# Tracing the merge's last gated sums ahead of the weight splits that follow them

## The chip, the cores and the metric

The kernel runs on one core of a Trainium2 chip. The metric is device time in microseconds (us), the median over several executions. One further execution is recorded by the profiler; its timeline is what "the trace" means below. The engines are PE (matrix multiply), DVE (vector), ACT (scalar), POOL, and SP, which here issues the transfers. Each works through its own queue in order.

## The reference, cut to what matters

Two layers over 256 tokens of width 1024, in float32. The part that the change touches is the merge of the two attention branches and the projection behind it:

```
branch_a = (o_gla * silu(gg)) @ w_o_gla
branch_b = gqa_attention(q, k, v) @ w_o_attn
mixed = sigmoid(gate_a) * branch_a + sigmoid(gate_b) * branch_b
h = h + rms_norm(mixed @ w_out, g_mix_post)
gate, up = split(rms_norm(h, g_ffn_pre) @ w_ffn_in, 2)
h = h + rms_norm((silu(gate) * up) @ w_ffn_out, g_ffn_post)
```

Each token half (`hf`, 128 tokens) and each column half (`j`, 512 columns) of `mixed` is one block of 128x512.

## The kernel before, in words

Weights stream through one pipeline (`Stream`, lines 214 to 324). A unit is 512 rows by 512 columns, 1 MB. SP loads it into one of two raw buffers. It is then split into a rounded high part (`wh`, a cast on ACT, line 113) and the rest (`wl`, a subtraction on DVE, line 109), each in two pieces of 128x1024; the two parts have four places each. A matrix product is three matmuls, high by high, high by low and low by high (`mm3`, line 99). `ws.take()` hands the next split unit to the matmuls. `ws.done()` gives its place back and, through `fill` (line 309), at once traces the split of the next loaded unit and the load behind it: two casts, two subtractions, and the transfers into the raw buffer that the split frees.

The merge runs over the steps in `MERGE` (line 39). Its last four steps are the `w_o_gla` units: for column half j = 0 the row halves kh = 0 and 1, then the same for j = 1. One unit is 24 matmuls, 12 for hf 0 and then 12 for hf 1. After kh = 1 the function `merged` (line 1204) takes each half's sum from PSUM: a multiplication by the gate (line 106) and an addition of the other branch (line 1210), both 128x512 on DVE. For j = 1 it also makes a task that will transpose the block on PE (line 436) and split the transposed block for the next product (`transpose_in`, line 432: a cast on ACT, a subtraction on DVE). A task waits for a number of ticks, and a tick falls after every six matmuls; here the number is `WAIT_MIX` = 3.

Next comes the product with `w_out` (`by_half`, line 662), first all of hf 0 and then all of hf 1. Its four units are called out 0 to out 3 here: (kh 0, j 0), (kh 0, j 1), (kh 1, j 0), (kh 1, j 1). Out 0 and out 1 need the merged blocks with j = 0, out 2 and out 3 those with j = 1. With four places, out 0 and out 1 are split into the places of the first two gla units, and out 2 and out 3 into those of the last two. The splits of out 2 and out 3 bring the loads of the first two units of `w_ffn_in` with them, two transfers each.

The order on each engine is not the traced order as it stands. A planner goes over the traced instructions with a clock of its own, in which every instruction and transfer has an estimated duration, and gives each engine the instruction that is ready and was traced first. `tc.high_priority(AHEAD)` counts the instructions in its block as traced 400 places earlier. `tc.issue_after(x)` puts what its block traces on x's engine behind x in that engine's queue, and leaves other engines' instructions free.

Of the kernel before, what the change touches and what calls it, by code (L numbers as in the profile page):

```python
# [15 lines left out]
ALU = mybir.AluOpType  # L16
# [9 lines left out]
AHEAD, EMPTY, EMPTY_FIRST = 400, 100, 1600  # L26
# [25 lines left out]
def trunk_kernel(ctx: ExitStack, tc: tile.TileContext, a: dict, out: bass.AP):  # L52
# [7 lines left out]
    nc = tc.nc  # L60
# [23 lines left out]
    def acc():  # L84
        return accp.tile([P, 512], F32, tag="acc", name=nm("acc"))
# [19 lines left out]
    def vmul(out, in0, in1):  # L105
        nc.vector.tensor_tensor(out=out, in0=in0, in1=in1, op=ALU.mult)
# [107 lines left out]
    class Stream:  # L214
# [8 lines left out]
        def __init__(self, depth):  # L223
            self.depth, self.held, self.room, self.ready, self.open = depth, 0, 0, [], False
            self.loads, self.jobs, self.lend = [], [], False
            pairs = {}
            for item in plan:
                if callable(item):
                    x = Load(item)
                    self.loads.append(x)  # L230
                    self.jobs.append(lambda x=x: self.plain(x))
                else:
                    units, n = item
                    if n == 1:
                        b11, b12, b21, b22 = units
                        x, z = (Load(b, lambda tag=tag: self.lent(tag), tag == "wh") for b, tag in ((b11, "wh"), (b12, "wl")))
                        y, q = Load(b22, big), Load(b21)
                        pairs[id(units)] = x, y, z, q
                        self.loads += [x, y, z]
                    if n == 5:  # L240
                        self.loads.append(q)
                    self.jobs.append(lambda p=pairs[id(units)], n=n: self.step(n, *p))
# [83 lines left out]
    ws = Stream(4)  # L326
# [105 lines left out]
    def transpose_in(sp, src, k, n, hf, plain=None):  # L432

        ps = aux()
        for i in range(n):
            nc.tensor.transpose(ps[:, i * P : (i + 1) * P], src[:, i * P : (i + 1) * P], ident)
        with tc.high_priority(AHEAD):
            sp.put(ps[:, : n * P], k, n, hf * P, P)
        if plain is not None:
            nc.scalar.copy(plain, ps[:, : n * P])  # L440
# [100 lines left out]
    def amode(o, sp, hf, k0, w, first, last, c0=0):  # L541

        wh, wl = (t[:, :2048].rearrange("p (k c) -> p k c", c=512)[:, :, c0 : c0 + o.shape[-1]] for t in w)
        sp.need(hf, k0)
        for k in range(4):
            mm3(o, sp.tok(k0 + k, hf), (wh[:, k, :], wl[:, k, :]), first and k == 0, last and k == 3)
            if k % 2 and (k == 3 or o.shape[-1] == 512):
                tick()
# [95 lines left out]
    def project_t(sp):  # L644

        o = [acc(), acc()]
        for kh in range(2):
            wmode(o, sp, kh * 4, ws.take(), kh == 0, kh == 1)
            ws.done()
        return o  # L650

    def project(sp):

        o = [acc(), acc()]
        for kh in range(2):
            w = ws.take()
            for hf in range(2):
                amode(o[hf], sp, hf, kh * 4, w, kh == 0, kh == 1)
            ws.done()
        return o  # L660
# [74 lines left out]
    uT = Split()  # L735
# [71 lines left out]
    for l in range(DEPTH):  # L807
# [86 lines left out]
        o = {}  # L894
# [135 lines left out]
        for x in range(2):  # L1030
            o = project_t(uT)
# [143 lines left out]
        for j in range(2):  # L1175
            o = project(uT)
            for hf in range(2):
                nc.scalar.copy(gg[:, hf, j * 512 : (j + 1) * 512], o[hf])
        gT = Split()
# [21 lines left out]
        mixT, sgate, seen = Split(), [], set()  # L1201
        part_of = lambda br, hf, j: sgate[br][:, hf, j * 512 : (j + 1) * 512]

        def merged(br, hf, j, o):
            vmul(part_of(br, hf, j), o, part_of(br, hf, j))
            if (hf, j) not in seen:
                seen.add((hf, j))
                return
            y = part_of(0, hf, j)
            nc.vector.tensor_tensor(out=y, in0=y, in1=part_of(1, hf, j), op=ALU.add)  # L1210

            def turn():
                yield WAIT_MIX
                transpose_in(mixT, y, 4 * j, 4, hf)

            turn = turn() if j or hf == 0 else mixT.turn_words(y, 0, 4, hf)
            mixT.makers[hf].append(Task(turn, part[0], j))

        def units(sp, then):
            for j in range(2):  # L1220
                o = [acc(), acc()]
                for kh in range(2):
                    w = ws.take()
                    for hf in range(2):
                        amode(o[hf], sp, hf, kh * 4, w, kh == 0, kh == 1)
                    ws.done()
                    if kh == 1:
                        for hf in range(2):
                            then(hf, j, o[hf])
                    yield  # L1230

# [10 lines left out]
        def gated(hf, o0, o1):  # L1242
            merged(1, hf, 0, o0)
            merged(1, hf, 1, o1)

        gate_units, gla_units, seven_ = gates(), units(gT, lambda hf, j, o: merged(0, hf, j, o)), None
        for x in MERGE:
            if x == "g" and not ogate.over:
# [43 lines left out]
        for hf in range(2):  # L1292
            ws.lend = hf == 1
            for b in range(2):
                o = acc()
# [39 lines left out]
        o = []  # L1335
# [69 lines left out]
        for hf in range(2):  # L1405
            s = slice(hf * P, (hf + 1) * P)
            for j in range(2):
                o = acc()
# [35 lines left out]
        uT = nxt  # L1444
# [47 lines left out]
```

## Time and profile before

| | |
|---|---|
| time before, median of 3 | 925.68 us (925.47 to 928.27) |
| the profiled execution's own time | 931.57 us |
| its span, first to last instruction | 929.8 us |
| PE busy | 908.2 us, 98% of the span |
| DVE busy | 768.4 us, 83% |
| ACT busy | 642.7 us, 69% |
| mean granted clock of PE | 0.995 |
| share of the 16 DMA engines | 58.8% |

PE's busy time includes matmuls that run at a lower clock. A view of waits names the engine and the line that waited, what it waited for, and the time in total, how often, and the longest. A timeline row gives start, duration, engine, line, operation, output <- inputs, and in brackets the idle time before it with what ended it. In tile names the digit is the layer: `big_0gate` is the merged block of layer 0, `aux_0merge` its transposed copy in PSUM, `wl_0merge<-raw_0merge` a weight split traced in the merge.

### The profile page before, as it was taken

Reading aid. Unit: us, or ns where it says so; the run is one execution under the profiler, and the core shown is the slowest. Engines: PE = TensorE matmul, PEld = TensorE weight load, DVE = VectorE, ACT = ScalarE, POOL = GpSimd, SP = SyncE. Lnnn points to the kernel's source line nnn. Section 1 sums busy time; section 2 is a strip of 40 time slices with the busy share of each in tenths; the row PEclk is TensorE's granted clock in tenths of the full one; section 3 lists DMA queues with packets and bytes.
Section 4 is the critical chain, followed back from the end, with each engine's and each line's share of the span. In section 5 each row is a group of like instructions: output and inputs, shape, how many; then the busy total and the mean of one; then the engine's idle time right before and its main releaser. Section 6 shows DMA issues by size and latency. Waiting matters only on the chain.

```text
span 929.8 us, 12251 instructions
## 1 busy us (share of the span) xinstructions
PE 908.2 (98%) x4561; PEld 769.7 (83%) x4561; DVE 768.4 (83%) x963; ACT 642.7 (69%) x1032; POOL 87.7 (9%) x150
## 2 busy tenths in 40 slices
PE   8999999999899999999999999999989999999996
PEld 6999888888688887888899988888878788888786
DVE  4798978987578998998689789798785799979874
ACT  4668778864477787677765686777555788858563
POOL 2600211040010000000122002200001000000000
PEclk9999999999999999999999999999999999999999
DMA  6564456757477675847555524394583866665551
GB/s 227 173 213 149 137 176 230 156 187 241 132 232 230 175 257 173 290 145 242 173 181 182 183 89 155 119 270 157 206 257 111 283 206 222 212 249 169 181 182 46
DMA packets 117786, 176.60 MB, mean 190 GB/s; under 512 B 33047, under 2 KB 56087, under 8 KB 117726
## 3 DMA queue, kind: packets, MB, share of 16 engines
q1 hardware_dynamic: 117726, 175.81, 58.8%
q8 instruction: 36, 0.59, 0.3%
q14 instruction: 24, 0.20, 0.1%
HBM read 167.41 MB, written 1.05 MB: 181 GB/s over the span
## 4 chain that ended last, share of the span: by engine, by line
PE 58%; DVE 18%; DMA 10%; ACT 7%; issue 4%; POOL 2%; SPq 0%; ACTq 0%; POOLq 0%; DVEq 0%
PE acc_0ffnin L97 9%; PE acc_1ffnin L97 6%; PE acc_0ffnin L577 4%; DVE wl_1ffnin L109 4%; PE acc_1gate L97 4%; PE acc_1gqk L97 2%; PE acc_0rq L97 2%; PE acc_0gqk L97 2%; PE acc_1ple L97 2%; PE acc_1gg L97 2%; PE acc_1v L97 2%; PE acc_0v L97 2%; PE acc_0gg L97 2%; DVE wl_0merge L109 2%; DMA raw_1ffnin<-in_w_ffn_out_dram 2%
## 5 line engine op out<-in xcount | busy, mean ns | idle before, releaser
L97 PE MATMUL acc_1ffnin<-wh_1ffnin,big_1ffnin 128*128 128x512 f32 x176 | 56.3, 392 | 0.0
L97 PE MATMUL acc_0ffnin<-wh_0ffnin,big_0ffnin 128*128 128x512 f32 x176 | 56.2, 391 | 0.0
L113 ACT CAST wh_1ffnin<-raw_1ffnin 128x1024 fp32r<-128x1024 f32 x38 | 38.4, 1050 | 19.0 <-DMA raw_1ffnin<-in_w_ffn_out_dram 12.9
L109 DVE TENSOR_TENSOR wl_1ffnin<-raw_1ffnin,wh_1ffnin 128x1024 fp32r<-128x1024 f32 x38 | 45.1, 1222 | 7.9 <-ACT wh_1ffnin L113 7.9
L109 DVE TENSOR_TENSOR wl_0ffnin<-raw_0ffnin,wh_0ffnin 128x1024 fp32r<-128x1024 f32 x38 | 45.0, 1222 | 6.6 <-ACT wh_0ffnin L113 6.6
L113 ACT CAST wh_0ffnin<-raw_0ffnin 128x1024 fp32r<-128x1024 f32 x38 | 38.3, 1049 | 17.2 <-DMA raw_0ffnin<-in_w_ffn_out_dram 10.5
L97 PEld LDWEIGHTS acc_1ffnin<-wh_1ffnin,big_1ffnin 128*128 128x128 f32 x176 | 33.0, 188 | 7.0 <-DVE big_1ffnin L109 0.2
L97 PEld LDWEIGHTS acc_0ffnin<-wh_0ffnin,big_0ffnin 128*128 128x128 f32 x176 | 33.0, 188 | 6.9 <-DVE big_0ffnin L109 0.2
L113 ACT CAST wh_1ffnin<-lent_1ffnin 128x1024 fp32r<-128x1024 f32 x30 | 30.2, 1050 | 9.7 <-DVE lent_1ffnin L292 4.0
L109 DVE TENSOR_TENSOR wl_1ffnin<-lent_1ffnin,wh_1ffnin 128x1024 fp32r<-128x1024 f32 x30 | 35.4, 1222 | 1.3 <-ACT wh_1ffnin L113 1.3
L109 DVE TENSOR_TENSOR wl_0ffnin<-lent_0ffnin,wh_0ffnin 128x1024 fp32r<-128x1024 f32 x30 | 35.4, 1223 | 1.2 <-ACT wh_0ffnin L113 1.2
L113 ACT CAST wh_0ffnin<-lent_0ffnin 128x1024 fp32r<-128x1024 f32 x30 | 30.2, 1051 | 8.8 <-PE acc_0ffnin L97 3.4
L97 PE MATMUL acc_0ffnin<-wl_0ffnin,big_0ffnin 128*128 128x512 f32 x88 | 34.5, 392 | 0.3 <-DVE wl_0ffnin L109 0.2
L97 PE MATMUL acc_1ffnin<-wl_1ffnin,big_1ffnin 128*128 128x512 f32 x88 | 34.5, 393 | 0.1
L577 PE MATMUL acc_1ffnin<-wh_1ffnin,mid_1ffnin 128*128 128x512 f32 x96 | 31.0, 390 | 0.0
L577 PE MATMUL acc_0ffnin<-wh_0ffnin,mid_0ffnin 128*128 128x512 f32 x96 | 31.0, 390 | 0.0
L97 PE MATMUL acc_1ffnin<-wh_1ffnin,big_1wout 128*128 128x512 f32 x96 | 30.4, 389 | 0.0
L97 PE MATMUL acc_0ffnin<-wh_0ffnin,big_0wout 128*128 128x512 f32 x96 | 30.3, 389 | 0.0
L97 PE MATMUL acc_0rq<-wh_start,big_start 128*128 128x384 f32 (+1 forms) x96 | 25.2, 347 | 1.2 <-ACT big_start L124 1.2
L97 PE MATMUL acc_1rq<-wh_0ple,big_0ple 128*128 128x384 f32 (+1 forms) x96 | 23.4, 325 | 0.0
L577 PE MATMUL acc_1ffnin<-wh_1ffnin,big_1wout 128*128 128x512 f32 x72 | 23.1, 389 | 0.0
L577 PE MATMUL acc_0ffnin<-wh_0ffnin,big_0wout 128*128 128x512 f32 x72 | 23.1, 389 | 0.0
(741 smaller groups left out, 3027.3 us busy)
## 6 DMA issues: line engine op xcount, KB each, us to landing
raw_0ffnin<-in_w_ffn_out_dram SPq DMA_DIRECT2D x11, 1024.0 KB, 5.3
raw_1ffnin<-in_w_ffn_out_dram SPq DMA_DIRECT2D x11, 1024.0 KB, 5.7
lent_0ffnin<-in_w_ffn_in_dram SPq DMA_DIRECT2D x6, 1024.0 KB, 7.5
lent_1ffnin<-in_w_ffn_in_dram SPq DMA_DIRECT2D x6, 1024.0 KB, 7.5
raw_0rq<-in_w_in_dram SPq DMA_DIRECT2D x4, 1024.0 KB, 5.1
raw_0v<-in_w_in_dram SPq DMA_DIRECT2D x4, 1024.0 KB, 5.0
raw_0merge<-in_w_out_dram SPq DMA_DIRECT2D x4, 1024.0 KB, 5.8
raw_0wout<-in_w_ffn_in_dram SPq DMA_DIRECT2D x8, 512.0 KB, 4.7
```

What stands on the lines that cost most here:

```text
L97: return nc.tensor.matmul(o, lhsT, rhs, start=start, stop=stop)
L109: nc.vector.tensor_tensor(out=out, in0=in0, in1=in1, op=ALU.subtract)
L113: cast = nc.scalar.copy(hi, src)
L577: nc.tensor.matmul(o, x, y, start=first and k + n == 0, stop=k == 3 and n == 2, skip_group_check=not first)
```

## The change

For the second column half (j = 1) of the gla product, the multiplication and addition in `merged` are counted as traced 400 places earlier. `merged` returns the addition. `ws.done()` for the unit (kh 0, j 1) is no longer called after its own matmuls, but after hf 0's twelve matmuls of (kh 1, j 1) and hf 0's `merged`; the one for (kh 1, j 1) comes after hf 1's `merged`. Both are called under `issue_after` of the addition just traced, so the subtractions of out 2's split queue behind hf 0's addition, and those of out 3's split behind hf 1's. Hf 0's task is made twelve matmuls earlier, so its three ticks also begin twelve matmuls earlier. The gate units (`uT`) and j = 0 are traced as before.

```diff
         def merged(br, hf, j, o):
-            vmul(part_of(br, hf, j), o, part_of(br, hf, j))
+            y = part_of(0, hf, j)
+            with tc.high_priority(AHEAD) if br == 0 and j else nullcontext():
+                vmul(part_of(br, hf, j), o, part_of(br, hf, j))
+                if (hf, j) in seen:
+                    added = nc.vector.tensor_tensor(out=y, in0=y, in1=part_of(1, hf, j), op=ALU.add)
             if (hf, j) not in seen:
                 seen.add((hf, j))
                 return
-            y = part_of(0, hf, j)
-            nc.vector.tensor_tensor(out=y, in0=y, in1=part_of(1, hf, j), op=ALU.add)
...
             mixT.makers[hf].append(Task(turn, part[0], j))
+            return added
...
                     for hf in range(2):
                         amode(o[hf], sp, hf, kh * 4, w, kh == 0, kh == 1)
-                    ws.done()
-                    if kh == 1:
-                        for hf in range(2):
+                        if j and kh and sp is gT:
+                            with tc.issue_after(then(hf, j, o[hf]).ins):
+                                ws.done()
+                    if not j or sp is uT:
+                        ws.done()
+                        for hf in range(2 * kh):
                             then(hf, j, o[hf])
                     yield
```

## The prediction

> **What bounds the kernel now.** I read the waits of PE first, since PE is busy nearly all the time and any wait of PE that is left must be on the path to the end.
>
> ```profile
> core 0 of [0], span 929.8 us
> engine line waited for: us in total, times, longest us
> PE aux_0merge L436 <- DVE big_0gate L1210: 4.2, 2, 3.2
> PE aux_1merge L436 <- DVE big_1gate L1210: 3.0, 1, 3.0
> PE warm L124 <- POOL ident masks.py:199: 1.5, 1, 1.5
> ```
>
> The two largest waits are the ones that the change is about: the transposes (L436) wait for the addition (L1210) of the merge, in each layer. The list is sorted, so every other group of waits is 1.5 us or less, and that one lies at the start. Nothing of size stands later at which an earlier PE would be held up. Next I read PE's timeline at these places.
>
> ```profile
> 224.49 0.60 PE L436 MATMUL aux_0merge<-ident,big_0gate 128*128 128x128 f32 x4
> 224.85 0.48 PE L97 MATMUL acc_0merge<-wh_0merge,big_0gg 128*128 128x512 f32 x1
> 225.16 0.39 PE L97 MATMUL acc_0merge<-wl_0merge,big_0gg 128*128 128x512 f32 x1
> ...
> 231.76 0.39 PE L97 MATMUL acc_0wout<-wh_0merge,big_0merge 128*128 128x512 f32 x1
> ...
> 237.04 0.66 PE L436 MATMUL aux_0merge<-ident,big_0gate 128*128 128x128 f32 x4 [1.04 <-DVE big_0gate L1210]
> 240.89 1.05 PE L436 MATMUL aux_0merge<-ident,big_0gate 128*128 128x128 f32 x4 [3.19 <-DVE big_0gate L1210]
> ...
> 687.23 0.39 PE L97 MATMUL acc_1wout<-wh_1merge,big_1merge 128*128 128x512 f32 x1
> ...
> 691.32 0.60 PE L436 MATMUL aux_1merge<-ident,big_1gate 128*128 128x128 f32 x4
> 694.97 1.11 PE L436 MATMUL aux_1merge<-ident,big_1gate 128*128 128x128 f32 x4 [3.05 <-DVE big_1gate L1210]
> ```
>
> In layer 1, 18 matmuls of the `w_out` product start between 687.23 and 691.32: 4.09 / 18 = 0.227 us each. Then hf 0's block is transposed, and at the same tick hf 1's, which waits 3.05 us. Layer 0 waits 1.04 and 3.19. An undisturbed set of four transposes costs PE 0.44 us: from 224.49 two matmul steps end at 225.16, 0.67 later, of which one step of 0.227 is the matmul's own. The set at 240.89 takes 1.05 instead of 0.60, so something follows the wait, and the third view shows what. Its columns after the stretch are its length, the busy time (and count) of PE, PE's weight loads, DVE, ACT and POOL, then the granted clock, the DMA share and GB/s.
>
> ```profile
> 231.70:237.00 5.30, 4.30 (x19) 3.22 (x18) 4.18 (x6) 4.10 (x5) 0.00 (x0) 1.00 0.74 232
> 241.00:243.00 2.00, 2.00 (x7) 1.73 (x8) 0.84 (x2) 0.59 (x1) 0.00 (x0) 0.50 0.78 197
> 243.00:245.00 2.00, 2.00 (x7) 1.60 (x6) 0.29 (x1) 0.00 (x0) 0.00 (x0) 0.65 0.94 315
> 245.00:247.00 2.00, 2.00 (x10) 1.64 (x10) 0.00 (x0) 0.00 (x0) 0.00 (x0) 1.00 0.04 12
> 695.00:697.00 2.00, 2.00 (x7) 1.80 (x8) 1.38 (x3) 0.82 (x2) 0.00 (x0) 0.50 0.78 207
> 697.00:699.00 2.00, 2.00 (x7) 1.54 (x7) 0.43 (x1) 0.00 (x0) 0.00 (x0) 0.65 0.98 340
> ```
>
> After each long wait PE runs at half clock, and for a while counts as fully busy. The loss is 2 x 0.50 + 2 x 0.35 = 1.7 us a layer. The short wait of 1.04 us (first row) left the clock at 1.00. So the price of the stall is larger than the waits: 1.04 + 3.19 + 1.7 = 5.9 us in layer 0, 3.05 + 1.7 = 4.75 in layer 1, together **10.7 us**.
>
> Why is the addition late? DVE's queue in layer 0, and the end of it in layer 1:
>
> ```profile
> 232.82 2.36 DVE L109 TENSOR_TENSOR wl_0merge<-raw_0merge,wh_0merge 128x1024 fp32r<-128x1024 f32 x2 [2.29 <-ACT wh_0merge L113]
> 235.10 0.68 DVE L106 TENSOR_TENSOR big_0gate<-acc_0merge,big_0gate 128x512 f32<-128x512 f32 x1
> 235.70 0.68 DVE L109 TENSOR_TENSOR big_0merge<-t_0merge,big_0merge 128x512 fp32r<-128x512 f32 x1
> 236.30 0.69 DVE L1210 TENSOR_TENSOR big_0gate<-big_0gate,big_0gate 128x512 f32<-128x512 f32 x1
> 236.90 0.69 DVE L106 TENSOR_TENSOR big_0gate<-acc_0merge,big_0gate 128x512 f32<-128x512 f32 x1
> 237.87 2.36 DVE L109 TENSOR_TENSOR wl_0merge<-raw_0merge,wh_0merge 128x1024 fp32r<-128x1024 f32 x2 [0.28 <-ACT wh_0merge L113]
> 240.15 0.69 DVE L1210 TENSOR_TENSOR big_0gate<-big_0gate,big_0gate 128x512 f32<-128x512 f32 x1
> 240.75 0.69 DVE L109 TENSOR_TENSOR big_0merge<-aux_0merge,big_0merge 128x512 fp32r<-128x512 f32 x1
> ...
> 690.93 0.68 DVE L106 TENSOR_TENSOR big_1gate<-acc_1merge,big_1gate 128x512 f32<-128x512 f32 x1
> 691.95 2.36 DVE L109 TENSOR_TENSOR wl_1merge<-raw_1merge,wh_1merge 128x1024 fp32r<-128x1024 f32 x2 [0.34 <-ACT wh_1merge L113]
> 694.23 0.68 DVE L1210 TENSOR_TENSOR big_1gate<-big_1gate,big_1gate 128x512 f32<-128x512 f32 x1
> ```
>
> The first row is out 2's split. It waits 2.29 us for a cast, and hf 0's multiplication is queued behind it, although its sum was complete 13 matmul steps before 231.76 plus the last one's 0.39, at 229.2. Out 3's split (237.87, 691.95) stands between hf 1's multiplication and its addition.
>
> **The change, part by part.** *Nothing is added or removed* but order: the two casts, two subtractions and two loads of each `done()` move behind a pair of DVE operations of 0.68 and 0.69 us, which start every 0.60 us.
>
> *Hf 0's pair.* It can start at 229.2, or when DVE is free of out 1's split and one turned block (about 230.5, by the rows in the slower rival), and ends by 231.8. With the task made 12 matmuls earlier, its transposes are wanted six matmuls into `w_out`, at 231.76 + 6 x 0.227 = 233.1: 1.3 us of cover. The wait of 1.04 goes. Out 2's subtractions now stand behind the pair, but their cast holds them until 232.82 anyway: cost nothing.
>
> *Hf 1's pair.* Ready at 231.9. If the planner puts it ahead of out 2's split it ends by 233.3; if behind, it runs at 235.1 and ends at 236.4. Wanted at 231.76 + 18 x 0.227 + 0.44 = 236.3. Cost 0 to 0.1 us; the wait of 3.19 goes, and with it the half clock. In layer 1 the same places give the same.
>
> *What is late next.* Out 2 is used from 231.76 + 24 x 0.227 + 2 x 0.44 = 238.1, and its third matmul, at 238.5, is the first to need the low part of hf 0's turned block. In layer 1 these are 693.6 and 694.0. That write (the L109 row at 240.75) stands after out 3's split in the trace. Out 3's split cannot move forward: it waits for a cast that waits for its load.
>
> ```profile
> 236.79 1.99 ACT L113 CAST wh_0merge<-raw_0merge 128x1024 fp32r<-128x1024 f32 x2 [1.13 <-DMA raw_0merge<-in_w_out_dram]
> ...
> 253.26 1.03 ACT L113 CAST wh_0wout<-raw_0merge 128x1024 fp32r<-128x1024 f32 x1
> ```
>
> If the planner keeps that order, the write starts when the split ends (240.15 and 694.23) and lasts 0.69: done at 240.8 and 694.9, so PE waits 240.8 - 238.5 = **2.3 us** and 694.9 - 694.0 = **0.9 us**. If it puts the write ahead of the split, PE waits nothing. I take the first: with its pieces ready from the start of `w_out`, the split comes up on the planner's clock about as early as the transposes do, and the trace's order is the only row there is. Both ends stay for the range. Out 3 itself is in time: its split ends at 240.2 and it is used 12 matmuls after out 2, at 240.8 or later.
>
> *A residual wait and the clock.* Waits of 1.04 us (no loss) and of 3.05 (1.7 us lost) enclose the 2.3, so its clock price is between 0 and 1.7; I take 0, since the 2.3 falls apart into the wait for the turned block's high part and, two matmuls later, the one for its low part. The Trainium skill's "TensorE: Matmul & The Clock Gate", Part 1, says that the clock halves after an idle window of about 3.4 us, free-running. By that rule 2.3 us would seldom cost anything and the sum would stay as taken; but the 3.05 us row is under the skill's figure too and did trip, so the trace is the harsher of the two.
>
> *The moved loads.* Out 2's split frees the raw buffer for the next `w_ffn_in` unit, out 3's for the one after, two transfers each:
>
> ```profile
> 235.21 5.97 SPq L263 DMA_DIRECT2D raw_0merge<-in_w_ffn_in_dram  x4
> ```
>
> They start when the splits end, which do not move. They have landed by 245 (DMA share 0.04 from 245 on), and the first cast that reads them is at 253.26; with PE up to 5.9 us earlier that becomes 247.4. Cover 2.4 us at the worst. No other step is passed on SP, and POOL does nothing here (0.00 in the clock rows).
>
> *Sum.* 10.7 - 2.3 - 0.9 = 7.5 us less. The profiled execution would go from 931.57 to 924.1 (span 929.8 to 922.3). It ran 5.9 us above the median of the timed runs; I take the stall to be the same in those: 925.68 - 7.5 = **918.2 us**.
>
> **The rivals.**
>
> *All of it is won.* The planner places hf 0's turned write ahead of out 3's split. For it: that write counts as traced 400 places earlier. Against: it needs transposes and a cast first. 925.68 - 10.7 = 915.0.
>
> *The residual waits trip the clock in both layers.* For it: half clock after 3.05 us. Against: 1.04 did not. 918.2 + 3.4 = 921.6; it takes waits nearer 3 us.
>
> *It does nothing.* The stall only moves from the transposes to out 2, because the turned blocks come behind still more of DVE's or ACT's queue, or a later stage gives the time back. It would take 10.7 us of new waits. Against: the sorted list of waits leaves no later place, and the loads have cover. 925.7.
>
> *Slower: the pair holds up out 1's split.* The chain of waits shows what hangs on that split:
>
> ```profile
> 227.57 2.35 DVE wl_0merge L109 x2
> 229.93 0.30 DVE big_0merge L109
> 230.22 6.49 DMA raw_0merge<-in_w_out_dram
> ```
>
> Out 1's split ends at 229.92 and out 3's load starts right behind it. If the planner, with its 400 places, puts hf 0's pair ahead of that split, DVE stands until 229.2, the pair ends at 230.5 and the split at 232.8, 2.9 us later. Out 3 lands at 239.6, its split ends at 243.1, the turned write at 243.7: 5.2 us after it is wanted, plus 1.7 of clock, against 5.9 now. That is 1.0 us worse; in layer 1, 2.9 us on 694.9 is a wait of 3.8, plus 1.7, against 4.75: 0.75 worse. Time 927.4. It also makes `w_out`'s third matmul (232.2) wait 1.2 us for the block written at 229.93; if the clock falls there as well, 1.7 a layer more gives 930.8. It decides where the planner's clock has hf 0's sum ready before out 1's split. Against: in the trace out 1's split is placed ahead of a turned block that also counts 400 places earlier.
>
> **How the numbers follow.** Chances: forecast 0.40 (own range 916.5 to 920), all won 0.25, clock tripped 0.16, nothing 0.09, slower rival 0.10. The first three hold 0.81, from 915.0 to 921.6; with 1 us below and 2.4 above for the unknown places of the turned write in the two layers, the range is 914.0 to 924.0. About 0.3% (2.8 us) is what a measurement here can tell from no change. Faster by more than that: the first three less a hundredth, 0.80. Slower: 0.07, most of the slower rival, in its dearer form. Within: 0.13.
>
> **What would show it.** Right: no wait on the addition in the waits of PE; clock 1.00 throughout the `w_out` product; a wait of 2 to 2.5 us in layer 0 and about 1 in layer 1 at the first matmuls of out 2, for the turned block; on DVE the pair of hf 0 directly after out 1's split. Wrong: half clock still there, the turned write ahead of out 3's split (all won), out 3's load starting after 230.2 by more than a microsecond (slower rival), or a new wait of over 1.5 us behind the `w_out` product.

## The result and the profile after

The changed kernel runs in 919.17 us (median of 5 runs, 917.59 to 921.65) against 925.68 us (924.91 to 928.27) of the kernel before on the same chip: a ratio of **0.9927, 95% interval 0.9904 to 0.9949**. A second measurement beside other experiments gave 919.96 against 927.09, 0.9906 (0.9884 to 0.9928). The prediction was 918.2. Its number held; two of its terms did not, and they nearly cancel, which is luck; the experiments below take it apart.

The profiled execution of the changed kernel took 919.17 us. First its page, then the waits of PE, sorted by size:

```profile
span 917.5 us, 12250 instructions
...
PE 904.2 (99%) x4561; PEld 767.2 (84%) x4561; DVE 769.0 (84%) x963; ACT 643.6 (70%) x1032; POOL 85.9 (9%) x150
```

```profile
engine line waited for: us in total, times, longest us
PE warm L124 <- POOL ident masks.py:199: 1.5, 1, 1.5
PE aux_0ple L436 <- DVE mid_0ple L494: 0.8, 2, 0.5
```

The two waits on the addition, 4.2 and 3.0 us before, are gone, and no wait of the merge or of `w_out` stands in their place: the largest that is left was in the kernel before too, at its start. What became of the `w_out` product shows in its matmuls with the high half of the weights, where the numbers after the colon are the shortest, median and longest in ns, then the first and the last start. First before, then after, both layers each:

```profile
L97 PE MATMUL acc_0wout<-wh_0merge,big_0merge x80: 277/389/776, 231.8 to 261.8; 128*128 128x512 f32 x48, 128*128 128x256 f32 x32
L97 PE MATMUL acc_1wout<-wh_1merge,big_1merge x80: 277/389/774, 687.2 to 715.9; 128*128 128x512 f32 x48, 128*128 128x256 f32 x32
```

```profile
L97 PE MATMUL acc_0wout<-wh_0merge,big_0merge x80: 278/389/477, 230.6 to 254.4; 128*128 128x512 f32 x48, 128*128 128x256 f32 x32
L97 PE MATMUL acc_1wout<-wh_1merge,big_1merge x80: 278/389/478, 680.0 to 703.9; 128*128 128x512 f32 x48, 128*128 128x256 f32 x32
```

The stretch of `w_out` falls from 30.0 to 23.8 us in layer 0 and from 28.7 to 23.9 in layer 1: 6.2 + 4.8 = **11.0 us** in this pair of executions. The prediction put the whole stall at 10.7. The longest matmul falls from 776 to 477 ns: no half clock is left. The spans differ by 12.3 us; the remaining 1.3 includes 1.2 from before the first `w_out` matmul (231.8 to 230.6), where the order of work is not what this change is about and where the executions of all kernels here scatter from 228.9 to 231.9.

PE's timeline and the windows (PE, PE's weight loads, DVE, ACT, POOL, then granted clock, DMA share, GB/s) after:

```profile
230.63 0.39 PE L97 MATMUL acc_0wout<-wh_0merge,big_0merge 128*128 128x512 f32 x1
...
232.00 0.60 PE L436 MATMUL aux_0merge<-ident,big_0gate 128*128 128x128 f32 x4
...
235.19 0.60 PE L436 MATMUL aux_0merge<-ident,big_0gate 128*128 128x128 f32 x4
```

```profile
230.60:235.00 4.40, 4.40 (x23) 3.60 (x22) 4.17 (x5) 4.07 (x6) 0.00 (x0) 1.00 0.72 252
235.00:237.00 2.00, 2.00 (x12) 1.69 (x11) 0.58 (x1) 1.87 (x3) 0.00 (x0) 1.00 1.00 343
237.00:239.00 2.00, 2.00 (x10) 1.67 (x9) 2.00 (x3) 0.00 (x0) 0.00 (x0) 1.00 0.32 113
```

The two sets of transposes come 6 and 18 matmuls into `w_out`, each with its 0.60 us and no bracket of idle time, and PE is busy throughout at a clock of 1.00. DVE's queue, layer 0 and then the end of it in layer 1, and ACT's cast of out 3:

```profile
228.49 0.68 DVE L106 TENSOR_TENSOR big_0gate<-acc_0merge,big_0gate 128x512 f32<-128x512 f32 x1
229.20 0.69 DVE L1209 TENSOR_TENSOR big_0gate<-big_0gate,big_0gate 128x512 f32<-128x512 f32 x1
230.76 2.36 DVE L109 TENSOR_TENSOR wl_0merge<-raw_0merge,wh_0merge 128x1024 fp32r<-128x1024 f32 x2 [0.87 <-ACT wh_0merge L113]
233.04 0.69 DVE L106 TENSOR_TENSOR big_0gate<-acc_0merge,big_0gate 128x512 f32<-128x512 f32 x1
233.64 0.69 DVE L109 TENSOR_TENSOR big_0merge<-t_0merge,big_0merge 128x512 fp32r<-128x512 f32 x1
234.25 0.69 DVE L1209 TENSOR_TENSOR big_0gate<-big_0gate,big_0gate 128x512 f32<-128x512 f32 x1
236.41 0.69 DVE L109 TENSOR_TENSOR big_0merge<-aux_0merge,big_0merge 128x512 fp32r<-128x512 f32 x1 [1.48 <-ACT big_0merge L113]
237.02 2.35 DVE L109 TENSOR_TENSOR wl_0merge<-raw_0merge,wh_0merge 128x1024 fp32r<-128x1024 f32 x2
...
684.42 1.22 DVE L109 TENSOR_TENSOR wl_1merge<-raw_1merge,wh_1merge 128x1024 fp32r<-128x1024 f32 x1
685.59 0.69 DVE L109 TENSOR_TENSOR big_1merge<-aux_1merge,big_1merge 128x512 fp32r<-128x512 f32 x1
686.19 1.22 DVE L109 TENSOR_TENSOR wl_1merge<-raw_1merge,wh_1merge 128x1024 fp32r<-128x1024 f32 x1
```

```profile
233.90 2.00 ACT L113 CAST wh_0merge<-raw_0merge 128x1024 fp32r<-128x1024 f32 x2 [0.30 <-DMA raw_0merge<-in_w_out_dram]
...
245.92 1.03 ACT L113 CAST wh_0wout<-raw_0merge 128x1024 fp32r<-128x1024 f32 x1
```

Hf 0's pair now ends at 229.89, before `w_out` begins, with out 2's split behind it, not ahead. Hf 1's pair ends at 234.94, 0.25 us before its transposes. The turned write of hf 0 (236.41, and 685.59) stands ahead of out 3's split in layer 0 and between its two halves in layer 1. That is not where the prediction had put it.

### The profile page after: what moved, and what is told of

It reads as the page before. It is cut to its first block, busy times and chain, and to the rows that moved or that the text cites. A ratio compares the mean times of both kernels' runs of the same rounds, so it can differ in the third digit from the quotient of the medians.

```text
span 917.5 us, 12250 instructions
## 1 busy us (share of the span) xinstructions
PE 904.2 (99%) x4561; PEld 767.2 (84%) x4561; DVE 769.0 (84%) x963; ACT 643.6 (70%) x1032; POOL 85.9 (9%) x150
## 4 chain that ended last, share of the span: by engine, by line
PE 75%; DVE 11%; DMA 5%; ACT 4%; issue 3%; POOL 2%; SPq 0%; POOLq 0%; ACTq 0%; DVEq 0%
PE acc_0ffnin L97 10%; PE acc_1ffnin L97 6%; PE acc_1gate L97 5%; PE acc_0gate L97 5%; PE acc_0ffnin L577 4%; DVE wl_1ffnin L109 4%; PE acc_1gqk L97 3%; PE acc_0gqk L97 2%; PE acc_0rq L97 2%; PE acc_1ple L97 2%; PE acc_1gg L97 2%; PE acc_0gg L97 2%; PE acc_0v L97 2%; PE acc_1v L97 2%; PE acc_0merge L97 2%
## 5 line engine op out<-in xcount | busy, mean ns | idle before, releaser
L113 ACT CAST wh_0ffnin<-raw_0ffnin 128x1024 fp32r<-128x1024 f32 x38 | 38.3, 1050 | 17.4 <-DMA raw_0ffnin<-in_w_ffn_out_dram 10.8
L97 PE MATMUL acc_1ffnin<-wh_1ffnin,big_1wout 128*128 128x512 f32 x96 | 30.4, 389 | 0.0
```

The lines of the kernel that those rows point to most:

```text
L97: return nc.tensor.matmul(o, lhsT, rhs, start=start, stop=stop)
L113: cast = nc.scalar.copy(hi, src)
```

## The experiments

All medians are against runs of the kernel before on the same chip: 927.02 us for the first four experiments, 927.09 for the next four, 926.16 for the last two. The ratio and its interval compare all runs of the two kernels beside each other and are not the quotient of the two medians; the two differ most for the filled wait. The stretch is the one from the rows above, in layer 0 / layer 1.

| kernel | median us | ratio (95%) | stretch of `w_out` |
|---|---|---|---|
| before (profiled) | 925.68 | | 30.0 / 28.7 |
| changed | 919.17 | 0.9927 (0.9904 to 0.9949) | 23.8 / 23.9 |
| changed, again | 919.96 | 0.9906 (0.9884 to 0.9928) | 24.5 / 23.9 |
| priority only | 922.55 | 0.9945 (0.9925 to 0.9965) | 26.2 / 25.9 |
| trace order only | 923.67 | 0.9960 (0.9944 to 0.9977) | 26.2 / 26.1 |
| out 3 only | 922.62 | 0.9946 (0.9930 to 0.9961) | 25.5 / 25.6 |
| out 2 only | 927.46 | 1.0004 (0.9988 to 1.0020) | 30.8 / 26.2 |
| before, again | 927.28 | 0.9998 (0.9981 to 1.0015) | 30.4 / 28.9 |
| wait filled | 926.79 | 0.9977 (0.9963 to 0.9992) | 27.2 / 27.1 |
| turned write late | 920.71 | 0.9915 (0.9895 to 0.9935) | 24.2 / 25.1 |
| transposes as before | 921.95 | 0.9948 (0.9927 to 0.9968) | 26.8 / 25.9 |
| hf 1 transposed later | 922.31 | 0.9957 (0.9938 to 0.9975) | 27.9 / 26.0 |

**Priority only.** The kernel before, with the last pair's multiplication and addition under the priority of 400 places and `done()` left where it was:

```diff
-            vmul(part_of(br, hf, j), o, part_of(br, hf, j))
+            y = part_of(0, hf, j)
+            with tc.high_priority(AHEAD) if br == 0 and j else nullcontext():
+                vmul(part_of(br, hf, j), o, part_of(br, hf, j))
+                if (hf, j) in seen:
+                    nc.vector.tensor_tensor(out=y, in0=y, in1=part_of(1, hf, j), op=ALU.add)
...
-            y = part_of(0, hf, j)
-            nc.vector.tensor_tensor(out=y, in0=y, in1=part_of(1, hf, j), op=ALU.add)
```

> Only the 400 places of priority for the pair (multiplication and addition, j = 1); the calls of done() and the tasks stay where they were before. In the built program DVE's queue becomes in layer 0: first half of out 2's split, hf 0's multiplication, second half, hf 0's addition, hf 1's pair, out 3's split, both turned writes. Theory (the stall is DVE's queue order): laid on the rows of the kernel before, hf 0's addition ends at 236.4 and hf 1's at 238.3 against 235.85 and 236.9 wanted, so waits of about 2 us and no half clock in layer 0 (5.9 us lost before), about 2.3 us in layer 1 (4.75 before): some 6 us faster than before by those rows, 3 to 5 slower than the changed kernel. Rival (the gain comes from hf 0's earlier task and its earlier transposes on PE): no gain without them, 925.7 us.

Measured 922.55, 4.5 us under the kernel before and, by the ratios, 2 to 4 us short of the changed kernel's gain. The intervals overlap; the trace shows the gap too, with stretches 2.4 and 2.0 us longer than the changed kernel's. DVE in layer 0:

```profile
230.57 1.23 DVE L109 TENSOR_TENSOR wl_0merge<-raw_0merge,wh_0merge 128x1024 fp32r<-128x1024 f32 x1 [2.13 <-ACT wh_0merge L113]
231.72 0.68 DVE L106 TENSOR_TENSOR big_0gate<-acc_0merge,big_0gate 128x512 f32<-128x512 f32 x1
232.32 1.21 DVE L109 TENSOR_TENSOR wl_0merge<-raw_0merge,wh_0merge 128x1024 fp32r<-128x1024 f32 x1
233.45 0.68 DVE L1209 TENSOR_TENSOR big_0gate<-big_0gate,big_0gate 128x512 f32<-128x512 f32 x1
```

The multiplication goes between the halves of out 2's split and the addition behind them, not ahead of it: the waits on the additions are 1.1 and 1.8 us. So the priority by itself is worth over half of the gain, but it does not bring hf 0's pair in front of a split that was traced earlier.

**Trace order only.** The changed kernel without the priority and without the edge that keeps `done()` behind the addition:

```diff
-            with tc.high_priority(AHEAD) if br == 0 and j else nullcontext():
+            with nullcontext():
...
-                            with tc.issue_after(then(hf, j, o[hf]).ins):
-                                ws.done()
+                            then(hf, j, o[hf])
+                            ws.done()
```

> The changed kernel without the priority and without issue_after: done() still traced behind the pairs, hf 0's task still early, and the queues of PE, ACT, SP and POOL as in the changed kernel. DVE differs: half of out 2's split comes before hf 0's multiplication and the other half before its addition. Theory: hf 0's transposes are wanted at 233.1 on the rows of before, its addition ends at 236.5: a wait of 3.3 us and half clock, about 5 us lost in layer 0, and 1.3 + 1.5 us in layer 1: only 3 us of the gain is left, about 923. Rival (PE's order and the moved done() bring it): the same time as the changed kernel, 919.

Measured 923.67, 3.4 us less than before and, by the ratios, 3 to 5 us short of the changed kernel's gain. DVE goes half split, multiplication, half split, addition as in the first experiment, and PE waits, this time for longer, since its transposes come as early as in the changed kernel:

```profile
234.29 0.66 PE L436 MATMUL aux_0merge<-ident,big_0gate 128*128 128x128 f32 x4 [2.19 <-DVE big_0gate L1209]
```

The 2.19 us cost their own length and no more (stretch 26.2 against 23.8); the half clock that was expected in layer 0 did not come. The missing piece here is the **edge** from the addition to the split. With the edge there, the priority does nothing: the changed kernel built without its priority has the same order of instructions on all five engines.

**Out 3 only.** The changed kernel, but kh 0's `done()` of the last two units is called at once, so out 2's split may go first; kh 1's stays behind hf 1's addition. Hf 0's task, too, is made only after all the matmuls, as in the kernel before:

```diff
-                        if j and kh and sp is gT:
-                            with tc.issue_after(then(hf, j, o[hf]).ins):
+                    if j and sp is gT:
+                        if kh:
+                            then(0, j, o[0])
+                            with tc.issue_after(then(1, j, o[1]).ins):
                                 ws.done()
-                    if not j or sp is uT:
+                        else:
+                            ws.done()
+                    else:
                         ws.done()
```

> Out 2's split is traced where it was before (its place given back after its own matmuls) and hf 0's task is made after all matmuls; both pairs keep the priority, and only out 3's split queues behind hf 1's addition. Theory: the wait of about 3 us and the half clock were out 3's split standing before hf 1's addition, so most of the gain comes back: waits of 2 to 2.4 us in layer 0, 0.6 to 2.1 in layer 1, 920 to 921. Rival (out 2's split before hf 0's pair is what matters): near 925.

Measured 922.62, some 1.6 us above the upper end of what was expected, of which 1.3 is that the kernel before ran at 927.02 here and at 925.68 in the first comparison. The waits left are 0.8 us on the addition and 0.4 on the turned block in layer 0, and 0.4 and 0.6 on the same two in layer 1; the clock is 1.00 around all of them.

**Out 2 only.** The other half alone, as an edit of the changed kernel: out 2's split behind hf 0's pair, out 3's as before, ahead of hf 1's addition, and hf 1's pair without the priority:

```diff
-            with tc.high_priority(AHEAD) if br == 0 and j else nullcontext():
+            with tc.high_priority(AHEAD) if br == 0 and j and not hf else nullcontext():
...
-                            with tc.issue_after(then(hf, j, o[hf]).ins):
+                            if hf == 0:
+                                with tc.issue_after(then(hf, j, o[hf]).ins):
+                                    ws.done()
+                            else:
                                 ws.done()
+                                then(hf, j, o[hf])
```

> The other half: hf 0's pair early with priority, its task early, out 2's split queued behind it; for hf 1 the old order (done() traced first, no priority, no edge). DVE then has: hf 0's pair, out 2's split, hf 1's multiplication, first half of out 3's split, hf 0's turned write, second half, hf 1's addition. Theory: hf 1's addition ends at 241.9 (layer 0) and 696.0 (layer 1) against 236.3 and 691.75 wanted on the rows of before: waits of 5.6 and 4.3 us with half clock after each, 7.3 and 6.0 us lost against 5.9 and 4.75: slower than the kernel before by 2 to 3 us. Rival: half of the gain, 922.

Measured the same as before, 1.0004. It is neither the gain of the rival nor the loss of 2 to 3 us that the theory gave. PE in the two layers, and the windows that follow:

```profile
240.30 1.12 PE L436 MATMUL aux_0merge<-ident,big_0gate 128*128 128x128 f32 x4 [4.22 <-DVE big_0gate L1209]
...
694.21 0.66 PE L436 MATMUL aux_1merge<-ident,big_1gate 128*128 128x128 f32 x4 [2.20 <-DVE big_1gate L1209]
```

```profile
240.50:242.50 2.00, 2.00 (x8) 1.71 (x8) 0.77 (x2) 0.59 (x1) 0.00 (x0) 0.50 0.69 200
242.50:244.50 2.00, 2.00 (x6) 1.61 (x5) 0.26 (x1) 0.00 (x0) 0.00 (x0) 0.50 0.92 321
244.50:246.50 2.00, 2.00 (x7) 1.53 (x7) 0.00 (x0) 0.00 (x0) 0.00 (x0) 0.66 0.01 4
...
694.40:696.40 2.00, 2.00 (x12) 1.70 (x12) 1.05 (x2) 0.59 (x1) 0.00 (x0) 1.00 0.76 205
```

Hf 0's transposes no longer wait, so PE arrives sooner at hf 1's sum, which is no earlier (it ends 9.8 us after the first `w_out` matmul, 9.1 before): the wait of 1.04 + 3.19 becomes one of 4.22. In layer 1 the wait is 2.20 and costs no clock. The two layers show the price: 30.8 - 23.8 = 7.0 us in layer 0, of which 4.22 wait and 2 x 0.50 + 2 x 0.50 + 2 x 0.34 = 2.7 half clock after it; 26.2 - 23.9 = 2.3 us in layer 1, of which 2.20 wait. Moving out 2's split is worth nothing alone, even with hf 0's earlier transposes.

**Before, again.** The kernel before, unchanged, among the experiments.

> The kernel before, once more, with a profile of its own. The first profile of it ran 5.9 us above the median of its timed runs. Theory (the stall is the same in every execution, the surplus lies elsewhere): waits on the additions of about 4.2 and 3.0 us and half clock after both again. Rival (the stall differs from one execution to the next with the landing of out 3): smaller waits and a profile nearer to 926.

Measured 927.28, ratio 0.9998. The stall is there again:

```profile
240.19 1.11 PE L436 MATMUL aux_0merge<-ident,big_0gate 128*128 128x128 f32 x4 [4.06 <-DVE big_0gate L1210]
...
694.57 0.66 PE L436 MATMUL aux_1merge<-ident,big_1gate 128*128 128x128 f32 x4 [2.82 <-DVE big_1gate L1210]
```

Half clock follows both (0.50 from 239.4 to 243.4, and 0.73 then 0.50 from 694.6 to 698.6). But the profiled execution took 930.19 us, the longest of this experiment's 10 runs, as the 931.57 was longer than all five in its comparison. The timed runs differ in clock too: over the 64 of the kernel before beside the experiments, 39 had a mean granted clock of 0.995 or less (median 928.0 us) and 25 had 0.996 to 0.999 (median 926.3), while the changed kernel's had 0.997 or 0.998. So the profiled stall seems to be at the dear end of what the timed runs pay.

**Wait filled.** The kernel before, with 30 transposes of the identity, whose result nobody uses, issued where PE would stand and wait for hf 1's sum:

```diff
                 yield WAIT_MIX
+                if j and hf:
+                    warm = aux()
+                    for _ in range(30):
+                        nc.tensor.transpose(warm[:, 0:P], ident, ident)
                 transpose_in(mixT, y, 4 * j, 4, hf)
```

> The kernel before with 30 transposes of the identity, results unused, on PE between hf 0's and hf 1's transposes, some 2.7 us of work in a place where PE waits 3.1 us; nothing else is changed. Theory: the addition is no earlier, so PE still loses the 3 us, but its clock stays at 1.00: 1.7 us less per layer, 3.4 us faster than before. Rival (the half clock costs nothing on the path, or comes from something other than the wait): the same time as before.

Measured 0.9977, 2.1 us less (0.7 to 3.4 by the interval); the medians themselves lie only 0.3 us apart. The useless transposes took 3.44 us, not the 2.7 that was expected. The sum is still queued behind out 3's split, but it ends 7.8 and 6.6 us after the first `w_out` matmul in the two layers, about 1.2 us sooner than in the first profile of before (9.1 and 7.7), since out 3's cast came sooner. PE, then DVE's addition in each layer, and the windows behind it in layer 0:

```profile
234.39 0.64 PE L436 MATMUL aux_0merge<-ident,big_0gate 128*128 128x128 f32 x4
234.86 3.44 PE L1217 MATMUL aux_0merge<-ident 128*128 128x128 f32 x30
238.14 0.66 PE L436 MATMUL aux_0merge<-ident,big_0gate 128*128 128x128 f32 x4
...
688.55 3.44 PE L1217 MATMUL aux_1merge<-ident 128*128 128x128 f32 x30
691.83 0.60 PE L436 MATMUL aux_1merge<-ident,big_1gate 128*128 128x128 f32 x4
```

```profile
237.41 0.68 DVE L1210 TENSOR_TENSOR big_0gate<-big_0gate,big_0gate 128x512 f32<-128x512 f32 x1
...
689.91 0.69 DVE L1210 TENSOR_TENSOR big_1gate<-big_1gate,big_1gate 128x512 f32<-128x512 f32 x1
```

```profile
238.30:240.30 2.00, 2.00 (x12) 1.69 (x12) 1.08 (x2) 0.59 (x1) 0.00 (x0) 1.00 0.76 194
240.30:242.30 2.00, 2.00 (x10) 1.65 (x9) 0.00 (x0) 0.00 (x0) 0.00 (x0) 1.00 0.93 324
```

Hf 1's transposes are held up by 3.3 us in each layer, as long as waits that were followed by half clock, and the clock stays at 1.00; the stretches exceed the changed kernel's by 3.4 and 3.2 us, the holding alone. In layer 1 the useless work runs 1.2 us past the sum (690.60 to 691.83), so this edit gives a part of its gain away. That the half clock goes although hf 1's transposes are held up just as long shows it to be a price of its own. The timed runs agree in their clock: all ten have 0.997 to 0.999, where 12 of the 19 runs of the kernel before beside them have 0.995 or less. Its size in the timed runs is known only loosely, 2.1 us with 0.7 to 3.4 as the interval, against 3.4 in the profile before. By that, an estimate, some 3 to 6 us of the changed kernel's gain is left to the wait itself.

**Turned write late.** The changed kernel, with hf 0's transposing, and so its turned write, forced behind out 3's split, where the prediction had it. `last_sub[0]` is the subtraction traced last, so `held[1]` is the end of out 3's split:

```diff
+                            held.append(last_sub[0])
...
                 yield WAIT_MIX
-                transpose_in(mixT, y, 4 * j, 4, hf)
+                with tc.issue_after(held[1].ins) if j and not hf else nullcontext():
+                    transpose_in(mixT, y, 4 * j, 4, hf)
```

> The changed kernel with hf 0's turned write (DVE) queued behind out 3's split, as the forecast had assumed; the changed kernel has it ahead in layer 0 and between the two halves in layer 1. Theory: PE waits at the third matmul of out 2; 2.3 + 0.9 us by the landings of the first profile of before, 0.6 + 0.4 us by those of the profile of after. So 1 to 3 us slower than the changed kernel. Rival: no difference from the changed kernel, 919.

Measured 920.71 against 919.96 of the changed kernel on the same chip, 0.75 us more, with intervals that overlap:

```profile
235.95 2.36 DVE L109 TENSOR_TENSOR wl_0merge<-raw_0merge,wh_0merge 128x1024 fp32r<-128x1024 f32 x2 [0.20 <-ACT wh_0merge L115]
238.22 1.28 DVE L109 TENSOR_TENSOR big_0merge<-aux_0merge,big_0merge 128x512 fp32r<-128x512 f32 x2
```

The order is the predicted one, yet the split starts 4.1 us after this kernel's first `w_out` matmul (231.9), not 6.1 after it as in the kernel before (237.87 - 231.76), and PE waits nothing in layer 0; in layer 1 it waits 0.4 us on hf 1's addition and 0.4 for the turned block. So in the order that I had assumed, the predicted wait of 3.2 us was not there in this execution. "Transposes as before" shows below that it depends on when out 3 lands.

**The changed kernel again**, beside the last three:

> The changed kernel once more on the same chip as the runs beside it, with a profile of its own. Theory: no wait on the additions, clock 1.00 throughout the w_out product, 7 to 11 us below the kernel before. Rival (the first profile was a lucky one): waits of a microsecond or more at the transposes or at out 2.

Measured 919.96, ratio 0.9906; no wait at the merge or `w_out`. As the theory had it.

**Transposes as before.** The changed kernel with hf 0's set of transposes two ticks later, at the tick where the kernel before has it:

```diff
-                yield WAIT_MIX
+                yield WAIT_MIX + (2 if j and not hf else 0)
```

> The changed kernel, but hf 0's transposes are put back to where the kernel before has them on PE (two ticks more), next to hf 1's. DVE keeps both pairs ahead of out 2's and out 3's splits; hf 0's turned write falls behind out 3's split in both layers. Theory (the pairs' place on DVE is what matters): no wait at the transposes and no half clock; the turned write ends about 4.05 us after out 3's first cast starts, and out 2's third matmul wants it 6.8 us after the first w_out matmul, so with the casts at 3 to 5 us, as in the profiles so far, a wait of 0.3 to 2.3 us a layer: 1 to 3 us slower than the changed kernel, 920 to 922, clearly faster than before. Rival (the earlier transposes on PE are needed): most of the gain gone, 925.

Measured 921.95, 0.9948. The sums are early, but the two sets come together and the turned blocks are late. In layer 0:

```profile
238.32 0.51 PE L97 MATMUL acc_0wout<-wh_0merge,big_0merge 128*128 128x512 f32 x1 [1.50 <-ACT big_0merge L113]
...
239.88 0.73 PE L97 MATMUL acc_0wout<-wh_0merge,big_0merge 128*128 128x512 f32 x2 [0.83 <-DVE big_0merge L109]
```

About 2.5 us of the changed kernel's gain (0.9948 against 0.9927 and 0.9906, so 2 to 4) is not the sums but that hf 0's block is now transposed 12 matmuls ahead of hf 1's. The three kernels that mend DVE's order but keep the later transposes measured the same: priority only 0.9945, out 3 only 0.9946, and this one, with both edges, 0.9948. So the edges showed a gain over the priority only where hf 0 is also transposed earlier. And the waits above are the predicted ones: the turned write stands behind out 3's split here, out 3's cast starts 5.60 us after the first `w_out` matmul (235.79 - 230.19), and PE waits 1.50 + 0.83 = 2.3 us. In layer 1, with the cast at 3.50, it waits 0.7 us for the turned block, and 0.6 on hf 1's addition.

**Hf 1 transposed later.** The kernel before, with the sums as late as they were, and hf 1's transposes put off until the sum is there:

```diff
-                yield WAIT_MIX
+                yield 8 if j and hf else WAIT_MIX
```

> The kernel before with one number changed: hf 1's transposes come after 8 ticks instead of 3, inside hf 0's half of the w_out product, where hf 1's addition has long ended; nothing on DVE is reordered. Theory: the 3 us wait and the half clock go although the addition is as late as before; what is left is hf 0's wait of 1.0 us in layer 0 and waits of about 2.3 and 2.5 us for hf 0's turned write behind out 3's split: some 4.8 us faster than before by the first profile, about 4 in the timed runs: 922 to 923. Rival (the late additions hold up the stage wherever the transposes stand): 926 to 927.

Measured 922.31, 0.9957: 3.9 us won without touching DVE's queue. PE then waits for the turned block of hf 0 (0.18 and 1.44 us in layer 0, 1.4 in layer 1), which comes after out 3's split as before. So the stall can be halved from either end, by the place of its user or by that of its maker. No run with one alone had as good a ratio as the change, which moves the sums and, with hf 0's task, one of their users.

## Why the prediction was right, and where it was not

- **Why the addition is late** (it is queued behind splits on DVE): right. With the pairs ahead of the splits, both waits go; out 3's split is the one that decides (0.9946 alone), out 2's alone gives nothing. In layer 0, the prediction's first row of the clock stops at 237.00, just short of the end of the 1.04 us wait; the trace has 1.00 from there to 241 as well, so the reading holds.
- **The price of the stall, 10.7 us:** right in the profile, where the stretches differ by 11.0. That it holds a share of clock beside the waits was shown by the filled wait, with a size in the timed runs that is only loosely known.
- **Hf 0's pair** was to end by 231.8, with 1.3 us of cover: it ended at 229.89, since the pair went directly behind a turned block, at 228.49, and the transposes at 232.00 had 2.1. **Hf 1's pair** took the later of its two places, 4.3 us after the first `w_out` matmul, against 4.6 (236.4 - 231.76) that I had given it; 0.25 us to spare, cost 0 as taken.
- **What is late next, 2.3 + 0.9 us:** this step failed, with 0 measured. I had taken DVE's order and the load's arrival from the trace of before as they stood. The planner put the turned write ahead of out 3's split in layer 0 and between its halves in layer 1, the end that I had named and not chosen. And the load was early: out 3's cast starts 3.27 us after the first `w_out` matmul (233.90 - 230.63), against 5.03 before (236.79 - 231.76). A second trace of each gave 4.19 and 4.70, and over all the kernels profiled here it is 2.99 to 5.60 in layer 0; one trace's place of a DMA was taken as fixed. With the order forced and the cast at 2.99 the time rose by 0.75 us, within overlapping intervals; with the cast at 5.60 ("transposes as before") the 2.3 us of layer 0 were there. So the wait that I priced can occur, and the order of the changed kernel avoids it.
- **The moved loads:** right. They cost nothing. The first cast that reads them starts at 245.92, and no wait behind `w_out` is over 0.5 us.
- **"I take the stall to be the same in those":** this step failed as well. The gain in the profiles is 11.0 us; by the timed medians it is 6.5 (925.68 - 919.17) and 7.1 (927.09 - 919.96), and by the ratios 6.8 and 8.7. The intervals of the two ratios are 4.7 to 8.9 and 6.7 to 10.8 us, and 11.0 lies outside both. So most runs before seem not to pay the full stall, though no trace of such a run was kept. A part of that goes with the clock: the medians at low and high mean clock differ by 1.7 us. Why the executions that were profiled stand at the top of the timed ones (931.57 and 930.19) while those of the changed kernel do not (919.17, its median) stays open: no run varied that.
- **The sum.** 10.7 - 3.2 = 7.5 was forecast. It came out as 11.0 less 2.3 to 4.5 us of stall that the timed runs do not show: 6.5 to 8.7. That the number was right within about a microsecond is luck, one error of 3.2 us against another of about the same size. The mechanism was that of the rival "all of it is won" (no residual wait), whose 915.0 missed by the second error alone. By the signs that I had named, the waits on the addition and the half clock went as forecast; the waits at out 2 did not come, and the turned write ahead of out 3's split, in layer 0, was the sign for that rival.
- **The slower rival** did not come. Out 1's split stayed ahead of hf 0's pair, and the sums passed only the splits that they were meant to pass.

## What to carry to other kernels

When an engine waits for the last operation of a chain, look at what stands in front of that operation in its own in-order queue, and tie bulk work that has slack behind it with an explicit edge: with hf 0's transposes moved up, trace order without the edge gave about half of the gain here. With them left in place, the priority did as much as the edges, about two thirds. Move the consumer as well as the producer: either alone left 2 to 5 us. The stall's price in the profiled execution, 11.0 us with clock in it, was above what the timed runs gained here; and the place of out 3's cast moved by 0.9 us between two traces of one kernel and by 2.6 over all of them. Profile the kernel before twice before the sum is made to a microsecond.

## What the runs showed of the hardware that I had not expected

**The clock does not follow the length of a wait alone.** Single waits of 2.19 and 2.20 us left the clock at 1.00; those of 2.82, 3.05, 4.06 and 4.22 were followed by half clock, and so was the pair of 1.04 and 3.19, which lie 0.7 us apart. But "hf 1 transposed later" has only waits of 0.18 and 1.44 us in layer 0, and the clock fell:

```profile
236.00:238.00 2.00, 1.45 (x6) 0.53 (x4) 2.00 (x3) 0.84 (x2) 0.00 (x0) 1.00 0.65 218
238.00:240.00 2.00, 0.94 (x4) 0.80 (x5) 1.01 (x2) 0.00 (x0) 0.00 (x0) 0.96 0.38 109
240.00:242.00 2.00, 2.00 (x7) 1.52 (x6) 0.00 (x0) 0.00 (x0) 0.00 (x0) 0.50 1.05 339
```

"Transposes as before" leaves PE idle for longer in as long a stretch, and kept it:

```profile
236.00:238.00 2.00, 0.81 (x4) 0.33 (x2) 1.13 (x1) 2.00 (x3) 0.00 (x0) 1.00 0.72 251
238.00:240.00 2.00, 0.85 (x3) 0.42 (x4) 2.00 (x4) 0.75 (x2) 0.00 (x0) 1.00 0.03 10
240.00:242.00 2.00, 2.00 (x9) 1.65 (x10) 0.43 (x1) 0.00 (x0) 0.00 (x0) 1.00 0.68 196
```

Idle for 0.55 + 1.06 = 1.6 us of four the clock fell; idle for 1.19 + 1.15 = 2.3 us of four it did not. The Trainium skill's "TensorE: Matmul & The Clock Gate", Part 1, has the clock looked at in windows that run free of the work. That would let the same idle time fall on either side, and it fits these two; that the windows' phase is the cause was not tested. The Trainium skill's length of about 3.4 us for an idle window does not fit the 1.6. The half clock also lasts longer or shorter: 1.7 us were lost after the 3.19 us wait, 2.7 after the one of 4.22.

**Useless work on PE is not lost work.** Thirty transposes of the identity in a wait that was there anyway made the kernel 2.1 us faster by the ratio (0.7 to 3.4), and kept the clock of all its timed runs at 0.997 or above.
